# A seven-product matmul group: its running weight sum begun one group earlier, its third sum added on VectorE, and two blocks of small work given out in steps

## Chip, cores, metric

One core of a Trainium2 chip. The metric is the device time of one execution in microseconds (us). Before the change: 3050.57 us, the median of three runs (3047.31 to 3052.44).

## What is computed

Two consecutive layers of a decoder trunk on one sequence of 256 tokens, width 2048, in float32. What matters here, cut from the reference:

```python
h = x
for i in range(DEPTH):                       # 2 layers
    h = h + mixers[i](rmsnorm(h, attn_norms[i]))
    h = h + conv_ffn(rmsnorm(h, ffn_norm), w_up, conv_w, conv_b, w_down)
    h = h + ple_term(h, p[i], w_proj, gate_norm, w_gate)
return rmsnorm(h, final_norm)

def conv_ffn(hn, w_up, conv_w, conv_b, w_down):       # w_up (2048, 11264), w_down (5632, 2048)
    u = causal_dwconv(hn @ w_up, conv_w) + conv_b     # 3 taps over the tokens
    gate, up = jnp.split(u, 2, axis=-1)
    return (jax.nn.silu(gate) * up) @ w_down
```

Layer 0's mixer projects the normed input once and feeds two groups of heads: a gated delta rule, which needs per-head gates (`beta = sigmoid(b)`, `g = -exp(A_log) * softplus(a + dt_bias)` and its cumulative sums), and a latent attention, which needs a rotation table (`cos`, `sin` of positions times inverse frequencies). Layer 1's mixer is a retention. All weights are read once from HBM.

## The kernel before

**Matmuls.** A float32 product is made of float32r pieces: a 128x1024 piece of a weight is cast by ScalarE to `hi` (L186), VectorE makes `lo` = weight - `hi` (L187), and TensorE multiplies `hi` with both parts of the activation and `lo` with its high part. `load` (L162) brings 1 MB of weight with one or more DMAs on SP's queue into a tile of the pool `rawp`, which has four buffers (`RAWB`); `cut` (L174) makes `hi` and `lo` from it, in pools of four tiles each. A buffer comes free when both have been made. `gemm_b` (L250) makes a product with the weights stationary (L259, L264), `gemm_a` (L277) with the activations stationary (L288, L289, L294).

**Who orders the work.** The program is written as Python generators that yield after some matmuls each; `weave`, `turn` and the loops of the FFN interleave them. Small work is put in the queue `todo` with `later` (L207), and `turn` (L210), which each GEMM calls after every eight or sixteen matmuls, takes one entry from it; `behind` (L202) keeps the entry's TensorE instructions behind the last matmul issued. A planner then sets the order in which each engine's instructions stand, by this order as priority and by what is ready in its own simulation; it also gives out the buffers. On the chip each engine, SP's and GpSimd's DMA queues too, goes through its instructions in that fixed order and waits at each for its inputs and its buffer.

**The FFN** (`ffn`, L1021) cuts the 44 tiles of 128 hidden channels into six groups: 4, 8, 8, 8, 8, 8. For each group `up` makes the gate and the up-projection (`conv`: two `gemm_b` of 2 MB of `w_up` per pair of tiles) and writes their product into `xg` tiles, four for a group of eight (`xtile`, L120; the pool has 18). `down` then multiplies the group with its 1024 rows of `w_down` and adds into `h`. `down` of one group runs as filler inside `up` of the next: `up` gets a lead of `LAG` = 6 steps, and then `down` makes 0.85 steps for each of `up`. The last group's `down` runs alone.

For the four middle groups of each FFN, half of `down` (512 columns twice) is done by `seven` (L390): one level of Winograd's form of Strassen's algorithm. The 256 tokens, the group's 1024 hidden channels and the 1024 columns are each halved, and instead of eight products of halves there are seven, over sums of weight blocks and sums of activation blocks (`Forms`, L362). Call the weight blocks B11, B12 (upper half) and B21, B22 (lower half). Their sums are made by DMA: `put` (L394) copies a block, `plus` (L398) issues from GpSimd a DMA that adds a block to what is in the tile. Each is two DMAs of 512 KB.

- A *running sum* `run_t` lives in two `xg` tiles. `put` B11 and `plus` B12 come at the start of `seven` (L433, L434), which `down` reaches after the lead (`next(fast)`, L1071). Product one reads it; `plus` B22 (L440), product four reads it; `plus` B21 (L449), product seven reads it.
- The *third sum* `t3` takes a buffer of `rawp` (L450): `put` B12 and `plus` B22. Product six reads it.
- Products two, three and five read plain blocks (`fresh`, L406): B11, B21 and B22.

The other half of `down` (columns 1024 on) is the ordinary `gemm_a` (`slow`, L1072); one step of it alternates with two of `seven`.

**The start.** The last 1104 columns of layer 0's input projection are made in three GEMMs, `g3` = 0, 1, 2 (L619). At `g3` = 1 the positions, the gates' parameters and the constants are loaded. At `g3` = 2 the program issues, all at once and ahead of that GEMM: the gates (`gates`, L564), the norm of the compressed queries (`low_rank`, L609), and the rotation tables (`rope_tables`, L467). The transposes of the compressed queries (`gained`, L308) are queued as the third turn of that GEMM.

Of the kernel before, what the change touches and what calls it, by code (L numbers as in the profile page):

```python
# [21 lines left out]
P = 128  # L22
# [29 lines left out]
C_QN = 96  # L52
# [32 lines left out]
def trunk(ctx: ExitStack, tc: tile.TileContext, a: dict):  # L85
# [121 lines left out]
    def later(*steps):  # L207
        todo.extend(steps)

    def turn():  # L210
        if todo:
            behind(todo.popleft())
# [174 lines left out]
                return self.hi[q][n // 2][:, n % 2, k], self.lo[q][n // 2][:, n % 2, k]  # L387
            return at

    def seven(w, r0, c, tiles, forms):  # L390

        blocks = w[r0 : r0 + 8 * P, c * 512 : (c + 2) * 512].rearrange("(q h k p) (e n) -> q h e p k n", q=2, h=2, k=2, e=2)

        def put(dst, hh, e):  # L394
            for q in range(2):
                nc.sync.dma_start(dst[q], blocks[q, hh, e])

        def plus(dst, hh, e):  # L398
            for q in range(2):
                G.dma_start(dst[q], blocks[q, hh, e], accum_op=ALU.add)  # L400

        def slab():
            raw = rawp.tile([P, 4, 512], F32, tag="raw", name=nm("raw"))
            return [raw[:, 2 * q : 2 * q + 2] for q in range(2)]

        def fresh(hh, e):  # L406
            dst = slab()
            put(dst, hh, e)
            return dst

        def x(half, i):
            def at(q, k):
                return xl(tiles, 4 * q + 2 * half + k, i)
            return at

        def product(o, left, right, start):
            los = []
            for q in range(2):
                hi, lo = cut(right[q], 2, 512)
                los.append(lo)  # L420
                for k in range(2):
                    l = left(q, k)
                    T.matmul(o, l[0], hi[k], start=start and q + k == 0, stop=False, skip_group_check=True)  # L423
                    last_mm[0] = T.matmul(o, l[1], hi[k], start=False, stop=False, skip_group_check=True)  # L424
                yield
            for q in range(2):
                for k in range(2):
                    last_mm[0] = T.matmul(o, left(q, k)[0], los[q][k], start=False, stop=q + k == 2, skip_group_check=True)
            yield

        h11, h12, h21, h22 = h[0][c], h[0][c + 1], h[1][c], h[1][c + 1]
        run_t = [xtile().bitcast(F32).rearrange("p a b c -> p a (b c)") for _ in range(2)]
        put(run_t, 0, 0)  # L433
        plus(run_t, 0, 1)  # L434
        yield
        one = pb()
        yield from product(one, forms.left(0), run_t, True)
        V.tensor_sub(h22, h22, one)
        V.tensor_sub(h12, h12, one)
        plus(run_t, 1, 1)  # L440
# [12 lines left out]
        one = pb()  # L453
        yield from product(one, forms.left(3), fresh(1, 1), True)
        V.tensor_sub(h12, h12, one)
        yield from product(acc, forms.left(2), t3, False)
        V.tensor_sub(h22, h22, acc)
        V.tensor_add(h21, h21, acc)
        one = pb()
        yield from product(one, x(1, 1), run_t, True)  # L460
        V.tensor_add(h21, h21, one)

    def put_split(t, k, n, src):
# [1 line left out]
        V.tensor_sub(t[:, k : k + n, 1], src, t[:, k : k + n, 0].bitcast(F32))  # L465

    def rope_tables(inv, cos, sin, sign):  # L467
        big = 2.0 * math.pi * 4096.0
# [17 lines left out]
        turns_of(m, big)  # L486
        take(m, wide[:3])
        turns_of(n, 2.0 * math.pi)
        take(n, turn)
        take(m, wide[3:])  # L490
        turns_of(n, 2.0 * math.pi)
        take(n, turn)
        pi = 3.1415925
        V.tensor_scalar(ang, ang, pi, -pi, op0=ALU.min, op1=ALU.max)
        A.activation(sin, ang, AF.Sin)
        if sign is not None:
# [67 lines left out]
    def gates():  # L564
        def hh(t):
            return t.rearrange("p h i -> p i h")

        def sm():
            return small(16).rearrange("p (i h) -> p i h", i=NH)

        bl = ab[:, :, 8:16]
        e = sm()
        V.scalar_tensor_tensor(e, bl, -1.0, bl, op0=ALU.mult, op1=ALU.min)
        A.activation(e, e, AF.Exp)
        V.tensor_scalar(e, e, 1.0, None, op0=ALU.add)
# [4 lines left out]
        V.tensor_mul(hh(beta), num, e)  # L580
        x = sm()
# [4 lines left out]
        A.activation(e, na, AF.Exp)  # L586
        u = sm()
# [9 lines left out]
        V.scalar_tensor_tensor(lg, x, 0.0, lg, op0=ALU.max, op1=ALU.add)  # L597
        ea = small(8)
# [5 lines left out]
        T.matmul(ps[:, 16:32], M["sl"], gf, start=True, stop=True)  # L604
        A.activation(eg.rearrange("p h i -> p (h i)"), ps[:, 0:16], AF.Exp)
        A.activation(kdx.rearrange("p h i -> p (h i)"), ps[:, 16:32], AF.Exp)
        V.scalar_tensor_tensor(nbe, beta, -1.0, eg, op0=ALU.mult, op1=ALU.mult)
# [11 lines left out]
    for g3 in range(3):  # L619
        if g3 == 1:  # L620
# [5 lines left out]
            V.tensor_copy(posf, posi)  # L626
# [394 lines left out]
    def ffn(l, nf, nxt, aside=None):  # L1021
# [32 lines left out]
                        forms.add(*kept)  # L1054
                        kept = []

        def down(g0, g1, tiles, forms):
            r0, nk = g0 * P, g1 - g0

            def plain(cols):  # L1060
# [18 lines left out]

        groups = [(max(g - 4, 0), g + 4) for g in range(0, NFT, 8)]  # L1080
        prev = None
        for g0, g1 in groups:
# [362 lines left out]
```

## Time and profile before

| | |
|---|---|
| profiled execution: device time | 3052.88 us |
| its span (first to last instruction) | 3051.1 us |
| median of three runs | 3050.57 us |
| TensorE busy | 2925.1 us (96%) |
| VectorE / ScalarE / GpSimd busy | 2054.3 / 1540.0 / 141.3 us |
| mean granted TensorE clock | 0.976 |
| moved by DMA | 570.88 MB, mean 187 GB/s |
| the two FFNs' stretches with seven-product groups | about 667 to 1260 and 2313 to 2900 us |

In the profile PE is TensorE's matmuls, PEld its weight loads, DVE VectorE, ACT ScalarE, POOL GpSimd; SPq and POOLq are the DMA-issuing sequencers. An operand `hi<-xg` means that a tile of the pool `hi` was written from one of `xg`. In a timeline row the numbers are start and length in us; in brackets stands how long the engine was idle before, and what ended that. The granted clock is 1 or one half; a mean between them is a mixture.

### The profile page before, as it was taken

The numbers are of one execution on the slowest core, as the hardware profiler recorded it, in microseconds if no ns is written. First come the engines' busy times: TensorE is split into PE (matmuls) and PEld (weight loads), VectorE is DVE, ScalarE is ACT, GpSimd is POOL, SyncE is SP. The second block draws the span as 40 slices with busy tenths as digits, with TensorE's granted clock in tenths as the row PEclk, the third lists the DMA queues.
The fourth block names the chain that finished last, engine by engine and source line by source line (L and its number), as shares of the span: only waits on it lengthen the run. The fifth ranks groups of instructions, "written<-read, shape, count | busy, mean of one in ns | idle before, by whom it ended". The sixth has DMA issues, their size and how long they took to land.

```text
span 3051.1 us, 38714 instructions
## 1 busy us (share of the span) xinstructions
PE 2925.1 (96%) x15076; PEld 2489.3 (82%) x15076; DVE 2054.3 (67%) x2882; ACT 1540.0 (50%) x2185; POOL 141.3 (5%) x132
## 2 busy tenths in 40 slices
PE   8999999999998999999999999999999999999998
PEld 8899988877777777888888888888887777777787
DVE  6888858767676766756655555666676767676664
ACT  6666645544454544554444444444555545445454
POOL 0111100000000000000000000000000000001000
PEclk9999999999999999999999999999999999999999
DMA  6444355567676767655555555555567677777654
GB/s 207 144 126 135 121 194 193 189 177 207 196 219 192 214 195 212 199 180 188 182 182 183 195 182 187 180 183 187 180 194 206 192 209 204 204 210 204 203 180 152
DMA packets 414392, 570.88 MB, mean 187 GB/s; under 512 B 11008, under 2 KB 267136, under 8 KB 414208
## 3 DMA queue, kind: packets, MB, share of 16 engines
q1 hardware_dynamic: 393376, 530.05, 53.7%
q0 software_dynamic: 17408, 33.56, 6.5%
q10 hardware_dynamic: 3424, 4.79, 0.5%
q8 instruction: 118, 1.93, 0.3%
q14 instruction: 66, 0.54, 0.0%
HBM read 566.26 MB, written 2.10 MB: 186 GB/s over the span
## 4 chain that ended last, share of the span: by engine, by line
PE 86%; DMA 7%; DVE 4%; ACT 2%; issue 1%; POOL 0%; ACTq 0%; POOLq 0%; SPq 0%; DVEq 0%
PE pa L259 26%; PE pa L264 13%; PE pa L288 10%; PE pa L294 10%; PE pa L289 10%; DMA xg<-in_l_ffn_w_down_dram 3%; DMA raw<-in_l_ffn_w_up_dram 3%; DVE lo L187 2%; PE pb L289 2%; PE pb L288 2%; PE pb L294 2%; PE pb L423 2%; PE pb L704 2%; PE pb L424 1%; ACT hi L186 1%
## 5 line engine op out<-in xcount | busy, mean ns | idle before, releaser
L187 DVE TENSOR_TENSOR lo<-raw,hi 128x1024 fp32r<-128x1024 f32 (+3 forms) x1140 | 1194.4, 1075 | 668.3 <-ACT hi L186 420.6
L186 ACT CAST hi<-raw 128x1024 fp32r<-128x1024 f32 (+3 forms) x1140 | 1014.6, 930 | 1010.3 <-PE pa L289 326.6
L259 PE MATMUL pa<-xg,hi 128*128 128x512 f32 x3840 | 975.4, 400 | 45.6 <-ACT hi L186 45.6
L259 PEld LDWEIGHTS pa<-xg,hi 128*128 128x128 f32 x3840 | 724.5, 193 | 200.2 <-ACT hi L186 54.4
L288 PE MATMUL pa<-hi,xg 128*128 128x512 f32 (+1 forms) x1348 | 524.2, 389 | 5.1 <-ACT hi L186 5.0
L264 PEld LDWEIGHTS pa<-xg,lo 128*128 128x128 f32 x3840 | 495.0, 191 | 33.0 <-DVE lo L187 13.0
L289 PE MATMUL pa<-hi,xg 128*128 128x512 f32 (+1 forms) x1348 | 521.6, 387 | 0.3 <-DVE xg L313 0.2
L264 PE MATMUL pa<-xg,lo 128*128 128x256 f32 x3840 | 514.6, 284 | 0.2
L294 PE MATMUL pa<-lo,xg 128*128 128x512 f32 (+1 forms) x1348 | 332.7, 387 | 0.0
L288 PEld LDWEIGHTS pa<-hi,xg 128*128 128x128 f32 x1348 | 254.4, 189 | 55.0 <-ACT hi L186 5.9
L289 PEld LDWEIGHTS pa<-hi,xg 128*128 128x128 f32 x1348 | 254.4, 189 | 48.9 <-DVE xg L313 0.8
L294 PEld LDWEIGHTS pa<-lo,xg 128*128 128x128 f32 x1348 | 249.8, 188 | 47.6
L1039 DVE SCALAR_TENSOR_TENSOR t<-t,fp,t 128x255 f32<-128x255 f32 (+1 forms) x352 | 159.5, 480 | 61.5 <-ACT t L1037 57.7
L288 PE MATMUL pb<-hi,xg 128*128 128x512 f32 x348 | 139.8, 402 | 0.0
L289 PE MATMUL pb<-hi,xg 128*128 128x512 f32 x348 | 139.6, 401 | 0.0
L1037 ACT ACTIVATE t<-t,fp 128x256 f32<-128x256 f32 x176 | 96.0, 593 | 74.6 <-DVE t L274 74.6
L271 ACT COPY t<-pa 128x512 f32<-128x512 f32 x128 | 74.9, 585 | 94.9 <-PE pa L264 85.6
L400 POOL DMA_DIRECT2D xg<-in_l_ffn_w_down_dram x48 | 57.9, 1207 | 1284.5 <-DMA xg<-in_l_ffn_w_down_dram 559.7
L187 DVE TENSOR_TENSOR lo<-xg,hi 128x1024 fp32r<-128x1024 f32 x48 | 58.0, 1223 | 84.9 <-ACT hi L186 61.9
L423 PE MATMUL pb<-hi,t 128*128 128x512 f32 x128 | 57.1, 446 | 55.0 <-ACT hi L186 55.0
L156 POOL TENSOR_TENSOR small<-small,mhalf 128x1 f32<-128x1 f32 (+2 forms) x38 | 28.7, 754 | 1440.4 <-DVE small L1214 622.5
L186 ACT CAST hi<-xg 128x1024 fp32r<-128x1024 f32 x48 | 49.5, 1047 | 88.4 <-DMA xg<-in_l_ffn_w_down_dram 58.5
(281 smaller groups left out, 2335.3 us busy)
## 6 DMA issues: line engine op xcount, KB each, us to landing
raw<-in_l_ffn_w_up_dram SPq DMA_DIRECT2D x176, 1024.0 KB, 5.6
raw<-in_l_w_in_dram SPq DMA_DIRECT2D x128, 1024.0 KB, 5.2
raw<-in_l_ffn_w_down_dram SPq DMA_DIRECT2D x56, 1024.0 KB, 5.2
raw<-in_l_w_out_dram SPq DMA_DIRECT2D x44, 1024.0 KB, 5.2
raw<-in_l_ffn_w_down_dram SPq DMA_DIRECT2D x64, 512.0 KB, 5.6
raw<-in_l_ple_gate_dram SPq DMA_DIRECT2D x32, 1024.0 KB, 5.1
xg<-in_l_ffn_w_down_dram POOLq DMA_DIRECT2D x48, 512.0 KB, 7.3
xg<-in_l_ffn_w_down_dram SPq DMA_DIRECT2D x16, 512.0 KB, 6.1
```

The costliest lines, as they stand in the source:

```text
L186: last_cast[0] = A.copy(vo(hi)[:, c], vi(rk)[:, c])
L187: V.tensor_sub(vo(lo)[:, c], vi(rk)[:, c], vo(hi)[:, c].bitcast(F32))
L259: last_mm[0] = T.matmul(ps[:, j], wh, x2, start=first, stop=False)
L264: last_mm[0] = T.matmul(ps[:, j, :S], lo[k][:, j * P : (j + 1) * P], xr(tiles, c * 8 + k)[1], start=False, stop=c == 1 and k == 7)
L271: A.copy(u, ps[:, :, S:])
L288: T.matmul(o[i], xh, hi[k], start=begin and k0 + k == 0, stop=False)
L289: last_mm[0] = T.matmul(o[i], xw, hi[k], start=False, stop=False)
L294: last_mm[0] = T.matmul(o[i], xl(tiles, k0 + k, i)[0], lo[k], start=False, stop=end and k0 + k == nkb - 1)
L423: T.matmul(o, l[0], hi[k], start=start and q + k == 0, stop=False, skip_group_check=True)
L704: T.matmul(ps[:, u * P : (u + 1) * P], l[:, u], r[:, u], start=True, stop=True)
L1037: A.activation(y[:, j], u[:, j], AF.Identity, scale=fc(ct + 176), bias=fc(ct + 264))
L1039: V.scalar_tensor_tensor(y[:, j, lag:], u[:, j, : S - lag], fc(ct + (2 - lag) * 88), y[:, j, lag:], op0=ALU.mult, op1=ALU.add)
```

## The change

Four edits:

1. `run_t` becomes `total`, two `xg` tiles taken once per FFN and kept. Its `put` B11 and `plus` B12 for the next group are issued by a callback, `then`, at the end of `seven` for the present group, when product seven has been issued; in the plain first group, at its start. For the last group there is none.
2. `t3` is no longer made by an accumulating DMA. B12 is brought by a plain `fresh` after product five, and VectorE adds B22 to it, from the buffer that product five read.
3. `gates` and the rotation tables become generators with `yield`s; at `g3` = 1 they are put in `todo` in 5 and 9 steps (`stepwise`), with the copy of the positions between.
4. At `g3` = 2 the norm of the compressed queries becomes the first turn, and their transposes the sixth.

```diff
+    def stepwise(gen, n):
+        later(*[partial(next, gen, None)] * n)
...
+    class Quads:
+        def __init__(self, w, r0, c, total):
+            self.blocks = w[r0 : r0 + 8 * P, c * 512 : (c + 2) * 512].rearrange("(q h k p) (e n) -> q h e p k n", q=2, h=2, k=2, e=2)
+            self.c = c
+            self.total = total
+        def put(self, dst, hh, e):
+            for q in range(2):
+                nc.sync.dma_start(dst[q], self.blocks[q, hh, e])
+        def plus(self, hh, e):
+            for q in range(2):
+                G.dma_start(self.total[q], self.blocks[q, hh, e], accum_op=ALU.add)
+        def begin(self):
+            self.put(self.total, 0, 0)
+            self.plus(0, 1)
...
+    def running():
+        return [xtile().bitcast(F32).rearrange("p a b c -> p a (b c)") for _ in range(2)]
+
+    def seven(quads, tiles, forms, then):
...
-        run_t = [xtile().bitcast(F32).rearrange("p a b c -> p a (b c)") for _ in range(2)]
-        put(run_t, 0, 0)
-        plus(run_t, 0, 1)
-        yield
         one = pb()
         yield from product(one, forms.left(0), run_t, True)
...
-        plus(run_t, 1, 0)
-        t3 = slab()
-        put(t3, 0, 1)
-        plus(t3, 1, 1)
+        plus(1, 0)
         one = pb()
-        yield from product(one, forms.left(3), fresh(1, 1), True)
+        b22 = fresh(1, 1)
+        yield from product(one, forms.left(3), b22, True)
         V.tensor_sub(h12, h12, one)
+        t3 = fresh(0, 1)
+        for q in range(2):
+            V.tensor_add(t3[q], t3[q], b22[q])
         yield from product(acc, forms.left(2), t3, False)
...
         yield from product(one, x(1, 1), run_t, True)
+        then()
         V.tensor_add(h21, h21, one)
...
+            later(lambda: None, lambda: None)
+            stepwise(gates(), 5)
+            later(lambda: V.tensor_copy(posf, posi))
+            stepwise(rope_steps(cst[:, C_IMLA : C_IMLA + 1], cos_t, sin_t, cst[:, C_SIGN : C_SIGN + 1]), 9)
         if g3 == 2:
-            with tc.issue_after(last_cast[0].ins):
-                gates()
-                low_rank(cq)
             cqT = []
-            later(lambda: None, lambda: None, lambda: cqT.extend(gained(cq, C_QN)))
-            rope_tables(cst[:, C_IMLA : C_IMLA + 1], cos_t, sin_t, cst[:, C_SIGN : C_SIGN + 1])
+            todo.appendleft(partial(low_rank, cq))
+            todo.insert(5, lambda: cqT.extend(gained(cq, C_QN)))
...
             if forms is None:
+                then()
                 yield from plain(range(CG))
                 return
-            fast = seven(w_dn, r0, 0, tiles, forms)
-            next(fast)
+            fast = seven(quads, tiles, forms, then)
...
+        def following(g0):
+            if g0 + 8 < NFT:
+                if not total:
+                    total.extend(running())
+                quads.append(Quads(w_dn, g0 * P, 0, total))
+                quads[-1].begin()
...
-                behind_it = down(*prev)
+                behind_it = down(*prev, quads[-1] if quads else None, partial(following, g0))
```

More of the change, by code (lines that the diff above doesn't have):

```diff
@@ L388, in left, with fresh @@
             return at
-    def seven(w, r0, c, tiles, forms):
-        blocks = w[r0 : r0 + 8 * P, c * 512 : (c + 2) * 512].rearrange("(q h k p) (e n) -> q h e p k n", q=2, h=2, k=2, e=2)
-        def put(dst, hh, e):
+    class Quads:
[4 more added lines that the diff above has]
+        def put(self, dst, hh, e):
             for q in range(2):
-                nc.sync.dma_start(dst[q], blocks[q, hh, e])
-        def plus(dst, hh, e):
+                nc.sync.dma_start(dst[q], self.blocks[q, hh, e])
+        def plus(self, hh, e):
             for q in range(2):
-                G.dma_start(dst[q], blocks[q, hh, e], accum_op=ALU.add)
-        def slab():
+                G.dma_start(self.total[q], self.blocks[q, hh, e], accum_op=ALU.add)
+        def begin(self):
+            self.put(self.total, 0, 0)
+            self.plus(0, 1)
+        def fresh(self, hh, e):
             raw = rawp.tile([P, 4, 512], F32, tag="raw", name=nm("raw"))
[L404 to L408, printed above, removed]
-            return dst
+            dst = [raw[:, 2 * q : 2 * q + 2] for q in range(2)]
+            self.put(dst, hh, e)
+            return dst
+    def running():
+        return [xtile().bitcast(F32).rearrange("p a b c -> p a (b c)") for _ in range(2)]
+    def seven(quads, tiles, forms, then):
+        c, run_t, fresh, plus = quads.c, quads.total, quads.fresh, quads.plus
         def x(half, i):
@@ L439, in seven @@
         V.tensor_sub(h12, h12, one)
-        plus(run_t, 1, 1)
+        plus(1, 1)
         acc = pb()
@@ L467, in rope_tables, with rope_steps @@
     def rope_tables(inv, cos, sin, sign):
+        return run(rope_steps(inv, cos, sin, sign))
+    def rope_steps(inv, cos, sin, sign):
         big = 2.0 * math.pi * 4096.0
@@ L486, in rope_tables @@
         turns_of(m, big)
+        yield
         take(m, wide[:3])
+        yield
         turns_of(n, 2.0 * math.pi)
+        yield
         take(n, turn)
+        yield
         take(m, wide[3:])
+        yield
         turns_of(n, 2.0 * math.pi)
+        yield
         take(n, turn)
+        yield
         pi = 3.1415925
@@ L495, in rope_tables @@
         A.activation(sin, ang, AF.Sin)
+        yield
         if sign is not None:
@@ L580, in gates @@
         V.tensor_mul(hh(beta), num, e)
+        yield
         x = sm()
@@ L586, in gates @@
         A.activation(e, na, AF.Exp)
+        yield
         u = sm()
@@ L597, in gates @@
         V.scalar_tensor_tensor(lg, x, 0.0, lg, op0=ALU.max, op1=ALU.add)
+        yield
         ea = small(8)
@@ L604, in gates @@
         T.matmul(ps[:, 16:32], M["sl"], gf, start=True, stop=True)
+        yield
         A.activation(eg.rearrange("p h i -> p (h i)"), ps[:, 0:16], AF.Exp)
@@ L1055, in up, with down @@
                         kept = []
-        def down(g0, g1, tiles, forms):
+        def down(g0, g1, tiles, forms, quads, then):
             r0, nk = g0 * P, g1 - g0
@@ L1081, in ffn @@
         prev = None
+        total = []
+        def following(g0):
[4 more added lines that the diff above has]
+                quads[-1].begin()
+        quads = []
         for g0, g1 in groups:
```

1 line of the change is left out of this document (removed).

## The prediction

> **What bounds the kernel now.** I read the page first, then TensorE's waits, then the timeline around one wait of each kind. The page's first part says TensorE is the bound:
>
> ```profile
> PE 2925.1 (96%) x15076; PEld 2489.3 (82%) x15076; DVE 2054.3 (67%) x2882; ACT 1540.0 (50%) x2185; POOL 141.3 (5%) x132
> ...
> L187 DVE TENSOR_TENSOR lo<-xg,hi 128x1024 fp32r<-128x1024 f32 x48 | 58.0, 1223 | 84.9 <-ACT hi L186 61.9
> ```
>
> So a change that leaves TensorE's matmuls alone, as this one does, can win only the 4% in which TensorE stands still, and what a standstill costs afterwards. The waits of TensorE (total us, times, longest):
>
> ```profile
> PE pb L423 <- ACT hi L186: 55.0, 8, 7.6
> PE pa L259 <- ACT hi L186: 45.6, 8, 7.6
> PE pa L288 <- ACT hi L186: 5.0, 3, 2.0
> PE pb L308 <- DVE t L617: 2.8, 1, 2.8
> ```
>
> Two waits come eight times each, once per seven-product group (four groups in each of two FFNs), 100.6 us together. Each is followed by slow matmuls. I asked for the 8 us after each of the sixteen restarts (columns: length, busy time and count of PE, PEld, DVE, ACT, POOL, granted clock, DMA share, GB/s); first two and last two of 16 rows:
>
> ```profile
> 673.61:681.61 8.00, 8.00 (x23) 6.32 (x24) 2.34 (x2) 3.23 (x4) 1.20 (x1) 0.62 0.49 75
> 746.09:754.09 8.00, 8.00 (x24) 6.38 (x25) 3.65 (x6) 3.97 (x5) 0.00 (x0) 0.67 0.02 6
> ...
> 2769.15:2777.15 8.00, 8.00 (x29) 6.38 (x30) 2.34 (x2) 4.33 (x5) 1.20 (x1) 0.82 0.45 74
> 2841.14:2849.14 8.00, 8.00 (x23) 6.21 (x24) 4.34 (x7) 3.86 (x6) 0.00 (x0) 0.62 0.01 3
> ```
>
> The sixteen clocks sum to 10.70, so (16 - 10.70) x 8 us = 42.4 us of matmul time is lost: 20.7 after the first kind (eight clocks sum to 5.41), 21.7 after the second (5.29). Both waits with their slow clock cost 143.0 us, 17.9 per group.
>
> **The first wait: the running sum.** The timeline shows it (start, length, engine, line, idle time before):
>
> ```profile
> 781.13 2.36 DVE L187 TENSOR_TENSOR lo<-xg,hi 128x1024 fp32r<-128x1024 f32 x2 [1.65 <-issue]
> ...
> 791.03 0.37 SPq L167 DMA_DIRECT2D raw<-in_l_ffn_w_up_dram  x1
> ...
> 797.34 4.23 SPq L167 DMA_DIRECT2D raw<-in_l_ffn_w_up_dram  x2
> ...
> 807.44 0.97 SPq L396 DMA_DIRECT2D xg<-in_l_ffn_w_down_dram  x2
> ...
> 813.09 1.19 POOL L400 DMA_DIRECT2D xg<-in_l_ffn_w_down_dram  x1 [81.68 <-DMA xg<-in_l_ffn_w_down_dram]
> ...
> 823.14 1.04 ACT L186 CAST hi<-xg 128x1024 fp32r<-128x1024 f32 x1 [7.54 <-DMA xg<-in_l_ffn_w_down_dram]
> ...
> 824.23 0.80 PE L423 MATMUL pb<-hi,t 128*128 128x512 f32 x1 [7.16 <-ACT hi L186]
> ```
>
> The old group's last reader of the sum ends at 781.13 + 2.36 = 783.49. The new sum is put by SP only at 807.44. It needs 5.65 us until POOL may add (813.09), then 10.05 until ScalarE casts (823.14). TensorE had run dry at 824.23 - 7.16 = 817.07. ScalarE waits in order, so the casts behind it stand too.
>
> The change issues both put and add when the old group's last product is through. If SP takes the put behind its next load (791.03 + 0.37), the cast can begin at 791.4 + 5.65 + 10.05 = 807.1, 8.9 us before it must (817.07 - 1.04 = 816.03). Even behind the two loads that end at 801.57 it begins at 817.3, 1.2 us late. So the wait goes: 55.0 + 20.7 us. The number of transfers of this sum is unchanged; they move some 16 us forward, into a stretch whose loads are issued at a pace of 3 to 7 us. For the first group of each FFN the sum is begun under the plain four-tile group, a whole group early. The two xg tiles stay taken between groups: 8 norm tiles, 4 and 4 product tiles and these 2 make 18, the pool's size, as now while a group runs; I price that at nothing, covered by the old product tiles coming free at the same end of group. Without that cover the next group's first pair would wait for the last low matmuls, at most one step.
>
> **The second wait: the third sum's slab.**
>
> ```profile
> 720.91 7.09 SPq L396 DMA_DIRECT2D raw<-in_l_ffn_w_down_dram  x4
> ...
> 725.50 2.44 POOL L400 DMA_DIRECT2D raw<-in_l_ffn_w_down_dram  x2 [0.50 <-DMA raw<-in_l_ffn_w_down_dram]
> ...
> 734.29 22.63 SPq L167 DMA_DIRECT2D raw<-in_l_ffn_w_up_dram  x3
> ...
> 735.54 1.05 ACT L186 CAST hi<-raw 128x1024 fp32r<-128x1024 f32 x1 [1.80 <-DMA raw<-in_l_ffn_w_down_dram]
> ...
> 744.99 2.94 ACT L186 CAST hi<-raw 128x1024 fp32r<-128x1024 f32 x3 [5.81 <-DMA raw<-in_l_ffn_w_up_dram]
> ...
> 746.09 2.08 PE L259 MATMUL pa<-xg,hi 128*128 128x512 f32 x4 [5.69 <-ACT hi L186]
> ...
> 760.57 0.69 DVE L455 TENSOR_TENSOR t<-t,pb 128x512 f32<-128x512 f32 x1 [0.35 <-PE pb L428]
> ...
> 762.18 0.39 PE L423 MATMUL pb<-hi,t 128*128 128x512 f32 x1
> ```
>
> SP issues four halves from 720.91: the third sum's first block, then the block of product four. The third sum takes one of four raw buffers at 720.91 though its product starts at 762.18. So the next w_up load gets a buffer only at 734.29 and, among POOL's accumulating transfers, lands after 10.7 us (744.99). TensorE had run dry at 740.40.
>
> After the change the block of product four takes 720.91. That w_up load then takes the turn that the second pair of the four has now (they end at 720.91 + 7.09 = 728.00), about 727, and the accumulating transfer of 1 MB is gone. Even with 10.7 us it lands at 738, and with the 5.65 of above at 733: in time for 740.40 less a cast. The third sum's plain load comes two loads later, about 741, and lands by 752, before VectorE gets to it; the stretch before is shorter by the first wait, so by this measure VectorE gets there about 751. It is tight, and I take the wait as gone: 45.6 + 21.7 us.
>
> What comes in its place are sixteen adds of 128x1024. The subtraction of the page's second row is the same shape: 1.22 us each, 2.4 per group. They lie on VectorE:
>
> ```profile
> 673.61:824.23 150.62, 137.73 (x692) 115.56 (x692) 104.49 (x136) 73.95 (x91) 9.57 (x8) 0.94 0.71 203
> 2400.00:2450.00 50.00, 50.00 (x270) 42.63 (x270) 38.94 (x47) 27.38 (x33) 0.00 (x0) 1.00 0.68 222
> 500.00:550.00 50.00, 50.00 (x288) 44.21 (x289) 44.49 (x76) 28.40 (x38) 0.00 (x0) 1.00 0.57 188
> ```
>
> A group of 150.6 us becomes 150.6 - 17.9 = 132.7, and VectorE 106.9 of it, 81%; it has been 89% busy with TensorE full (third row). The DMA moves 150.62 us x 203 GB/s = 30.6 MB less 1.05, or 222 GB/s, what the second row carries without a gap. Neither becomes the bound on average.
>
> The adds can still stand in a chain. If VectorE takes them behind the subtraction at 760.57, ScalarE's cast can start at 760.57 + 0.69 + 1.22 (2.44 if the first cast waits for both adds), and TensorE's product at 763.5 (764.7) instead of 762.18: 1.4 (2.6) us idle. Behind the adds on VectorE wait the low parts of the w_up tiles, needed some microseconds later. If the adds slip ahead of the subtraction, it is zero. A short gap may or may not slow the clock:
>
> ```profile
> 62.47 0.69 PE L308 MATMUL pb<-ident,t 128*128 128x128 f32 x2 [2.83 <-DVE t L617]
> ...
> 62.47:70.47 8.00, 8.00 (x43) 7.94 (x44) 5.88 (x13) 3.88 (x10) 0.00 (x0) 0.82 0.38 121
> 93.00:101.00 8.00, 8.00 (x48) 7.16 (x48) 5.61 (x14) 6.22 (x12) 0.00 (x0) 1.00 0.44 134
> ```
>
> After 2.83 us the clock was 0.82 for 8 us (1.4 us lost), after the gap before 93.00 (VectorE's, 2.0 us) it was whole. So the bounds are 0 and 2.6 + 1.4 = 4.0 us per group; I take 0.7 (half of the shorter chain, as the order is open), 5.6 us in all. The Trainium skill ("TensorE: Matmul & The Clock Gate", HAM oscillation) counts only gaps above about 3.4 us as harmful to the clock. The 2.83 us row disagrees; by the rule the upper bound would be 2.6 and the sum's upper end 11 us lower.
>
> **Gates and tables in steps.** Today the chain into the wait at 62.47 is this:
>
> ```profile
> 58.13 1.28 ACT L605 ACT_TABLE_LOAD   x1
> ...
> 61.92 0.88 DVE L617 TENSOR_SCALAR t<-t,small 128x512 f32<-128x512 f32 x2 [0.82 <-POOL small L156]
> ...
> 66.39 1.52 PE L294 MATMUL pa<-lo,xg 128*128 128x368 f32 x8
> ...
> 70.42 1.51 PE L294 MATMUL pa<-lo,xg 128*128 128x368 f32 x8
> ```
>
> The gates come wholly before the tables, so this table load leaves the chain (1.28 us), and the transposes come three turns later, a step of 70.42 - 66.39 = 4.0 us. Together they cover 2.83 us: with the clock 4.3 us are won. No instruction is added. The gates' own matmuls move up about 6 us; if TensorE meets them before VectorE's result, up to that is lost (with the clock 7). Bounds: a gain of 9 (the 5.0 us of L288 partly too) and a loss of 3 net. I take 4.3, because the wait of 2.83 is the row that the moved steps touch.
>
> **Sum.** The profiled execution took 3052.9 us (span 3051.1), 2.3 above the median of 3050.6. 3052.9 - 143.0 - 4.3 + 5.6 = 2911.2, or 2909 as a median.
>
> **Rivals.**
> 1. *The second wait stays* at its size, because product four's block is now held until the adds and the buffers are as scarce. For it: three buffers are left for everything else in that stretch, and the load of the third sum lands close to need. Against: the starved w_up load moves ahead by a turn. 3052.9 - 55.0 - 20.7 - 4.3 = 2973, median 2971.
> 2. *The first wait stays*: SP takes the put as late as now, behind loads that wait for buffers (the row at 807.44 speaks for it); against, that the put can be issued four SP loads earlier. 3052.9 - 45.6 - 21.7 - 4.3 + 5.6 = 2987, median 2985.
> 3. *Slower*: the adds stop VectorE. If the third sum's put gets a buffer only when VectorE has reached the adds, VectorE waits for it to land (the row of four issues ends at 728.00, the cast of the last pair's first half starts at 735.54: 7.5 us), adds and casts 2.3, less 1.6 that TensorE has left: 8.2. Meanwhile no low part is made and no buffer freed, so the next w_up load comes late like today's, 10.7. With two slow restarts of 2.65: 24.2 us per group, 3052.9 - 143.0 - 4.3 + 194 = 3099, median 3097. It decides for slower from (143.0 + 4.3) / 8 = 18.4 us per group. Against: four buffers let SP run about two loads ahead.
> 4. *Nothing*: both transfers stay where they are in their queues and the waits keep their size: about 3050.
>
> **Chances.** Forecast 0.72. Its own range ends above at 2909 + 32 - 5.6 (the add chains) + 4.3 + 2.7 (the start's loss) = 2942. Below, the start gives 4.7 more, the adds 5.6, and the gaps between matmuls may close a little; their pitch is in these rows:
>
> ```profile
> 657.82 2.08 PE L264 MATMUL pa<-xg,lo 128*128 128x256 f32 x16
> ...
> 659.74 3.82 PE L259 MATMUL pa<-xg,hi 128*128 128x512 f32 x16
> ...
> 663.39 0.39 PE L288 MATMUL pb<-hi,xg 128*128 128x512 f32 x1
> ```
>
> (659.74 - 657.82) / 16 = 0.120 us for 256 columns, 3.65 / 16 = 0.228 for 512. A group's 692 matmuls (256 of the first kind in eight up-projections) take 256 x 0.120 + 436 x 0.228 = 130.1, 2.6 less than 132.7. Half of that in eight groups is 10 us: 2889. Rival 1 0.12, rival 2 0.07, rival 3 0.04, rival 4 0.05. For 8 in 10 the range reaches over the own range and rival 1: 2888 to 2975. This kernel's runs agree within 5 us, so 0.2% (6 us) is about what can be told: faster 0.72 + 0.12 + 0.07 = 0.91, same 0.05, slower 0.04.
>
> **What would show it.** Right: L423's wait in the list of TensorE's waits gone or near 0, and POOL's first add on the sum some 10 us or more before ScalarE's cast; L259's wait gone; a clock of 1.0 over both FFNs; groups of about 132 us; no accumulating transfer into raw; sixteen adds of 1.2 us. Wrong: a new wait of VectorE for the third sum's transfer, or a wait of L259 or L423 of over 3 us per group; L308 waiting for L617 still, or L603 waiting at all.

## The result, and the profile after

The changed kernel takes 2905.43 us (median of four runs, 2905.28 to 2905.79); the kernel before, on the same chip, 3051.51 (3047.31 to 3053.89). The ratio is 0.9523, interval 0.9506 to 0.9539: 146 us won. The forecast was 2909, range 2888 to 2975. The profiled execution of the changed kernel took 2905.5 us, span 2903.7. The edits shift the line numbers; of the names in the prediction, L259 is now L262, L264 is L267, L288 is L291, L294 is L297, L308 is L311, L423 is L438, L396 is L403, L400 is L407, L455 is L464, L617 is L645.

The first line of the page after:

```profile
PE 2879.7 (99%) x15076; PEld 2457.5 (85%) x15076; DVE 2067.7 (71%) x2898; ACT 1539.3 (53%) x2185; POOL 121.6 (4%) x116
```

TensorE does the same 15076 matmuls in 2879.7 us instead of 2925.1, and of the span 2903.7 - 2879.7 = 24.0 us are left over instead of 3051.1 - 2925.1 = 126.0. So of the 147.4 us between the two profiled executions 102.0 are standstill and 45.4 are matmuls that no longer run at the half clock. VectorE has sixteen instructions more, GpSimd sixteen fewer.

TensorE's waits after (total us, times, longest):

```profile
PE pa L291 <- ACT hi L186: 7.1, 2, 5.4
PE pb L726 <- DVE t L845: 1.6, 1, 1.6
PE pa L267 <- DVE lo L187: 1.2, 4, 0.4
```

Neither of the two waits that came eight times each (L423 and L259 before) is in the list. The only large one left, 5.4 us, is at the start of the program, and it is longer than what stood there before. The first FFN's stretch, after (columns: stretch, length, busy time and count of PE, PEld, DVE, ACT, POOL, granted clock, DMA share, GB/s), with one group's period in the first row:

```profile
759.95:892.11 132.16, 132.07 (x694) 111.53 (x693) 106.28 (x138) 73.84 (x90) 7.19 (x6) 1.00 0.75 223
667.00:1260.00 593.00, 592.19 (x3048) 497.85 (x3047) 460.23 (x588) 329.63 (x418) 25.93 (x22) 1.00 0.72 215
```

and the same stretch before:

```profile
667.00:1260.00 593.00, 543.48 (x2714) 454.62 (x2713) 408.13 (x522) 290.64 (x352) 36.12 (x30) 0.94 0.71 203
```

TensorE stands still 0.8 us of 593, where it stood 49.5, and its clock is whole. A group has gone from 150.6 to 132.2 us; VectorE is busy 106.3 of them (80%), and the DMA moves 223 GB/s. The second FFN, which now starts earlier, looks the same (after):

```profile
2253.00:2766.00 513.00, 512.17 (x2674) 431.92 (x2674) 411.27 (x528) 285.00 (x351) 24.07 (x20) 1.00 0.75 221
```

The timeline of the changed kernel shows how both sums arrive (start, length, engine, line, idle time before):

```profile
706.57 0.89 SPq L403 DMA_DIRECT2D raw<-in_l_ffn_w_down_dram  x2
712.70 7.63 SPq L167 DMA_DIRECT2D raw<-in_l_ffn_w_up_dram  x2
724.96 0.88 SPq L403 DMA_DIRECT2D raw<-in_l_ffn_w_down_dram  x2
...
729.27 1.22 DVE L467 TENSOR_TENSOR raw<-raw,raw 128x1024 f32<-128x1024 f32 x1 [0.30 <-DMA raw<-in_l_ffn_w_down_dram]
730.65 1.22 DVE L467 TENSOR_TENSOR raw<-raw,raw 128x1024 f32<-128x1024 f32 x1 [0.16 <-DMA raw<-in_l_ffn_w_down_dram]
...
739.05 0.68 DVE L464 TENSOR_TENSOR t<-t,pb 128x512 f32<-128x512 f32 x1
...
740.28 0.39 PE L438 MATMUL pb<-hi,t 128*128 128x512 f32 x1
...
758.70 2.36 DVE L187 TENSOR_TENSOR lo<-xg,hi 128x1024 fp32r<-128x1024 f32 x2 [1.97 <-issue]
...
759.95 1.50 SPq L403 DMA_DIRECT2D xg<-in_l_ffn_w_down_dram  x2
...
764.09 1.20 POOL L407 DMA_DIRECT2D xg<-in_l_ffn_w_down_dram  x1 [47.01 <-DMA xg<-in_l_ffn_w_down_dram]
...
790.06 1.05 ACT L186 CAST hi<-xg 128x1024 fp32r<-128x1024 f32 x1 [1.53 <-issue]
...
794.45 0.40 PE L438 MATMUL pb<-hi,t 128*128 128x512 f32 x1
```

From the top: product four's block is put at 706.57, and the next w_up load follows after 6.1 us. The third sum's plain load is issued at 724.96; VectorE adds to each half as it lands (729.27, 730.65), and TensorE begins product six only at 740.28, 8.4 us after the second add ends. The running sum: its last readers are the two subtractions from 758.70, and SP puts the first half of the next group's block at 759.95, when the first of the two has ended; GpSimd adds at 764.09, 26.0 us ahead of ScalarE's cast at 790.06.

### The profile page after: what moved, and what is told of

Read it like the earlier page. It is cut to its first block, busy times and chain, and to the rows that moved or that the text cites. A ratio compares the mean times of both kernels' runs of the same rounds, so it can differ in the third digit from the quotient of the medians.

```text
span 2903.7 us, 38666 instructions
## 1 busy us (share of the span) xinstructions
PE 2879.7 (99%) x15076; PEld 2457.5 (85%) x15076; DVE 2067.7 (71%) x2898; ACT 1539.3 (53%) x2185; POOL 121.6 (4%) x116
## 4 chain that ended last, share of the span: by engine, by line
PE 92%; DVE 4%; DMA 1%; issue 1%; ACT 1%; POOL 0%; SPq 0%; ACTq 0%; POOLq 0%; DVEq 0%
PE pa L262 28%; PE pa L267 15%; PE pa L291 10%; PE pa L292 10%; PE pa L297 10%; PE pb L292 2%; PE pb L291 2%; PE pb L297 2%; DVE lo L187 2%; PE pb L732 2%; PE pb L438 2%; PE pb L439 1%; PE pb L443 1%; PE pb L311 1%; DMA raw<-in_l_ffn_w_down_dram 1%
## 5 line engine op out<-in xcount | busy, mean ns | idle before, releaser
L262 PE MATMUL pa<-xg,hi 128*128 128x512 f32 x3840 | 950.8, 393 | 0.0
L262 PEld LDWEIGHTS pa<-xg,hi 128*128 128x128 f32 x3840 | 705.8, 188 | 146.5 <-ACT hi L186 8.3
L291 PE MATMUL pa<-hi,xg 128*128 128x512 f32 (+1 forms) x1348 | 523.5, 389 | 7.2 <-ACT hi L186 7.1
L267 PEld LDWEIGHTS pa<-xg,lo 128*128 128x128 f32 x3840 | 495.0, 191 | 34.6 <-DVE lo L187 14.6
L267 PE MATMUL pa<-xg,lo 128*128 128x256 f32 x3840 | 514.7, 284 | 1.5 <-DVE lo L187 1.2
L297 PE MATMUL pa<-lo,xg 128*128 128x512 f32 (+1 forms) x1348 | 332.6, 387 | 0.0
L291 PEld LDWEIGHTS pa<-hi,xg 128*128 128x128 f32 x1348 | 253.9, 188 | 56.9 <-ACT hi L186 7.7
L297 PEld LDWEIGHTS pa<-lo,xg 128*128 128x128 f32 x1348 | 249.8, 188 | 47.5
L292 PE MATMUL pb<-hi,xg 128*128 128x512 f32 x348 | 135.9, 390 | 0.0
L291 PE MATMUL pb<-hi,xg 128*128 128x512 f32 x348 | 135.7, 390 | 0.0
L407 POOL DMA_DIRECT2D xg<-in_l_ffn_w_down_dram x48 | 57.9, 1206 | 1185.4 <-DVE t L1067 395.5
L297 PE MATMUL pb<-lo,xg 128*128 128x512 f32 x348 | 92.4, 391 | 0.0
L275 DVE TENSOR_TENSOR t<-t,pa 128x512 f32<-128x512 f32 x128 | 87.1, 680 | 3.8 <-ACT t L274 3.8
L316 DVE SCALAR_TENSOR_TENSOR xg<-pb,par,xg 128x256 fp32r<-128x256 f32 x136 | 59.7, 479 | 35.9 <-ACT xg L315 35.5
```

Source lines behind the costliest of these rows:

```text
L262: last_mm[0] = T.matmul(ps[:, j], wh, x2, start=first, stop=False)
L267: last_mm[0] = T.matmul(ps[:, j, :S], lo[k][:, j * P : (j + 1) * P], xr(tiles, c * 8 + k)[1], start=False, stop=c == 1 and k == 7)
L275: V.tensor_add(u, u, ps[:, :, :S])
L291: T.matmul(o[i], xh, hi[k], start=begin and k0 + k == 0, stop=False)
L292: last_mm[0] = T.matmul(o[i], xw, hi[k], start=False, stop=False)
L297: last_mm[0] = T.matmul(o[i], xl(tiles, k0 + k, i)[0], lo[k], start=False, stop=end and k0 + k == nkb - 1)
```

## The experiments

Each kernel has its own runs of the kernel before beside it (medians 3049.8, 3049.5 and 3049.8 us on the three chips).

### The parts one by one

First the changed kernel again, and beside it, on one chip, one kernel with edit 1 alone (the sum a group ahead), one with edit 2 alone (the third sum on VectorE), one with edits 3 and 4 alone (steps). With edit 1 alone, the third sum is made as before:

```diff
+        t3 = fresh(0, 1)
+        for q in range(2):
+            G.dma_start(t3[q], quads.blocks[q, 1, 1], accum_op=ALU.add)
         one = pb()
-        b22 = fresh(1, 1)
-        yield from product(one, forms.left(3), b22, True)
+        yield from product(one, forms.left(3), fresh(1, 1), True)
         V.tensor_sub(h12, h12, one)
-        t3 = fresh(0, 1)
-        for q in range(2):
-            V.tensor_add(t3[q], t3[q], b22[q])
```

Edit 2 alone is the same exchange the other way round, made in the kernel before.

> The changed kernel itself, on the chip of the next three. 2905 us, both kinds of FFN wait at zero.

> The kernel before with the running sum begun a group ahead and nothing else changed (the third sum by accumulating DMA, gates and tables all at once). Theory, two waits with causes of their own: the first product's wait on the sum (55.0 us of idle time, 20.7 of slow clock) goes, the second (45.6 + 21.7) stays: 3051 - 76 = 2975 us. Rival, the first wait is also a rest in which the loads catch up, so the second grows by as much as the first was: over 3020 us. Rival, the DMA is simply full and both waits shrink in part: L423's wait still some 20 us.

> The kernel before with only the third sum changed: plain load after product five, two VectorE adds. Theory: the second wait goes (45.6 + 21.7 us) and the first stays: 3051 - 67 = 2984 us. Rival, the second wait is an echo of the first (buffers run down while the sum's transfers go first): L259 still waits 20 us or more, time over 3010.

> The kernel before with only the gates and rotation tables in steps. The prediction said 4.3 us of gain. Having seen the changed kernel's trace, theory now: the 2.8 us wait at 62 us goes with its slow clock, but the gates' two ScalarE table loads come ahead of the first casts of the second GEMM and a wait of about 5.4 us stands at 36 us instead of 1.9: a gain of 0 to 4 us, 3047 to 3051 us. Rival, the new wait at 36 us has to do with something else: it is absent here and the gain is 4 to 6 us.

Measured: the changed kernel 2905.96 us (ratio 0.9529, interval 0.9515 to 0.9544), edit 1 alone 2977.23 (0.9764, 0.9749 to 0.9778), edit 2 alone 2982.91 (0.9782, 0.9768 to 0.9797), the steps alone 3047.19 (ten runs; 0.9992, 0.9982 to 1.0001). Against 3049.83 before, they win 72.6, 66.9 and 2.6 us: 142.1 together, and the whole change wins 143.9. So the parts add up, and neither wait was hiding behind the other. The waits say the same. Edit 1 alone:

```profile
PE pa L262 <- ACT hi L186: 47.6, 9, 7.6
PE pa L291 <- ACT hi L186: 4.9, 3, 1.9
PE pb L311 <- DVE t L644: 2.8, 1, 2.8
```

Edit 2 alone:

```profile
PE pb L423 <- ACT hi L186: 52.9, 8, 7.8
PE pa L288 <- ACT hi L186: 4.0, 3, 1.9
PE pb L308 <- DVE t L618: 2.8, 1, 2.8
```

Each leaves the other's wait at its old size. The interval of the steps alone reaches to 1.0001: their 2.6 us can't be told from nothing by these runs.

### What made the third sum's slab cost 67 us

The old way did two things at once: it held a raw buffer from early on, and it sent accumulating transfers through the stretch in which TensorE waits for a w_up load. Two kernels take them apart. One is the changed kernel with its plain load issued early (buffer held, no accumulating transfer):

```diff
+        t3 = fresh(0, 1)
         b22 = fresh(1, 1)
         yield from product(one, forms.left(3), b22, True)
         V.tensor_sub(h12, h12, one)
-        t3 = fresh(0, 1)
         for q in range(2):
             V.tensor_add(t3[q], t3[q], b22[q])
```

The other is the changed kernel with accumulating transfers at the late place (no buffer held):

```diff
-        b22 = fresh(1, 1)
-        yield from product(one, forms.left(3), b22, True)
+        yield from product(one, forms.left(3), fresh(1, 1), True)
         V.tensor_sub(h12, h12, one)
         t3 = fresh(0, 1)
         for q in range(2):
-            V.tensor_add(t3[q], t3[q], b22[q])
+            G.dma_start(t3[q], quads.blocks[q, 1, 1], accum_op=ALU.add)
```

> The changed kernel, but the plain load of the third sum's first block is issued ahead of product five's block, where the third sum's slab was taken before; VectorE adds as changed, no accumulating DMA into it. Theory, the second wait came from a raw buffer taken long before its use: the wait of L259 is back with 4 to 7 us per group, 2905 + 45 to 67 = 2950 to 2972 us. Rival, it came from the accumulating DMA (1 MB more, and its place among the transfers): no wait, 2905 to 2910 us.

> The changed kernel, but the third sum is made by an accumulating DMA again, at its new late place. Theory (buffer taken long): no wait of L259 for a w_up load as before; the sum is complete about 11 to 13 us after its load is issued at 725 us, about 738, a cast before its use at 740.3, so 0 to 3 us per group, 2905 to 2940 us, and any wait is L423's, for the sum. Rival (accumulating DMA): the wait of L259 is back, 2950 us or more.

Measured: 2913.11 us for the early load (0.9551, 0.9537 to 0.9566) and 2908.85 for the late accumulating transfers (0.954, 0.9526 to 0.9554). Neither alone brings the 67 us back. The early load should have cost 44 to 66 us by the theory that the buffer decides, and costs some 7 (2913.11 - 2905.96, medians of two chips); that theory falls. Its rival, 2905 to 2910 us, is missed too, by 3 us. The accumulating transfers alone, at their new place, cost no more than some 3 us. That kernel changes two things at once, since the late place also frees the buffer early; none here sends them at the old place without holding a buffer.

The stretch with edit 1 alone, which has both (timeline; the first row is the third sum's put together with product four's):

```profile
711.85 7.08 SPq L403 DMA_DIRECT2D raw<-in_l_ffn_w_down_dram  x4
725.23 7.18 SPq L167 DMA_DIRECT2D raw<-in_l_ffn_w_up_dram  x2
...
735.83 2.94 ACT L186 CAST hi<-raw 128x1024 fp32r<-128x1024 f32 x3 [5.72 <-DMA raw<-in_l_ffn_w_up_dram]
...
736.93 2.07 PE L262 MATMUL pa<-xg,hi 128*128 128x512 f32 x4 [5.60 <-ACT hi L186]
```

and with the early plain load:

```profile
707.06 7.12 SPq L403 DMA_DIRECT2D raw<-in_l_ffn_w_down_dram  x4
720.44 16.68 SPq L167 DMA_DIRECT2D raw<-in_l_ffn_w_up_dram  x3
...
727.64 2.95 ACT L186 CAST hi<-raw 128x1024 fp32r<-128x1024 f32 x3 [2.32 <-DMA raw<-in_l_ffn_w_up_dram]
...
728.74 1.20 PE L262 MATMUL pa<-xg,hi 128*128 128x512 f32 x4 [2.20 <-ACT hi L186]
```

In both the w_up load is issued 13.4 us after the put (in the changed kernel 6.1), so the buffer is as late in the one as in the other. TensorE is dry at the same place, 736.93 - 5.60 - 711.85 = 19.5 us after the put, and 728.74 - 2.20 - 707.06 = 19.5. What differs is how long the load takes until ScalarE may cast: 10.6 us with accumulating transfers in its way, 7.2 without. 13.4 + 7.2 is 1.1 us past that point, 13.4 + 10.6 is 4.5, and the first cast's 1.1 us comes on top of both: 2.2 and 5.6, the waits in the rows.

Is it that they add, or that their bytes are in the way? A third kernel takes edit 1 alone and has GpSimd's transfers copy B22 into the tile, with the same bytes at the same place; its third sum is B22 alone instead of B12 + B22:

```diff
-            G.dma_start(t3[q], quads.blocks[q, 1, 1], accum_op=ALU.add)
+            G.dma_start(t3[q], quads.blocks[q, 1, 1])
```

> The kernel with only the running sum begun a group ahead (2977 us, second wait 47 us), but the two GpSimd DMAs into the third sum's slab copy B22 instead of adding it, so the third sum is B22 alone and the output is not the reference's: the same bytes at the same place, without the add. Theory, the late w_up load in that place took 10.5 us instead of 7.1 because accumulating transfers are in its way: the second wait falls to 0 to 2 us per group as with VectorE's adds, 2911 to 2930 us. Rival, the extra 1 MB at that moment is what delays it: wait of L259 unchanged, about 6 us per group, 2970 to 2980 us.

Measured: 2953.05 us (0.9687, 0.9671 to 0.9704), between the two expectations. Its stretch:

```profile
709.64 7.09 SPq L403 DMA_DIRECT2D raw<-in_l_ffn_w_down_dram  x4
723.03 19.20 SPq L167 DMA_DIRECT2D raw<-in_l_ffn_w_up_dram  x3
...
731.18 2.94 ACT L186 CAST hi<-raw 128x1024 fp32r<-128x1024 f32 x3 [3.26 <-DMA raw<-in_l_ffn_w_up_dram]
...
732.27 2.06 PE L262 MATMUL pa<-xg,hi 128*128 128x512 f32 x4 [3.14 <-ACT hi L186]
```

Again 13.4 us from put to load, and now 8.2 us to the cast. TensorE's waits at this line come to 28.1 us, against 47.6 with adding and 7.0 with the early plain load. So of the time that TensorE stands still here, about half is due to the second megabyte and half to its being added. In device time the second megabyte weighs more: copying in place of adding saves 24.2 us (2977.23 to 2953.05), and going on to the early load 39.9 (to 2913.11, some 2.6 of it from the steps, which only that kernel has; the three ran on three chips). The slow matmuls make the difference: TensorE is busy 2902.1 us with adding, still 2897.9 with copying, and 2881.9 with the early load. The transfers themselves differ likewise (DMA issues: how many, KB each, median us from issue to landing). Adding, in the kernel with edit 1 alone:

```profile
raw<-in_l_ffn_w_down_dram POOLq DMA_DIRECT2D x16, 512.0 KB, 10.6
```

Copying, the same bytes at the same place:

```profile
raw<-in_l_ffn_w_down_dram POOLq DMA_DIRECT2D x16, 512.0 KB, 7.5
```

Adding at the late place of the changed kernel:

```profile
raw<-in_l_ffn_w_down_dram POOLq DMA_DIRECT2D x16, 512.0 KB, 6.7
```

At the crowded place adding takes 3.1 us longer than copying; at the late place even adding takes only 6.7. The price is that of the place as much as of the kind.

### How much room the adds have

The adds were priced at 0.7 us per group. Two kernels give VectorE more of them: each add is followed, once or twice, by a subtraction and an add of the same block: three or five passes over the tile in place of one. With five:

```diff
         for q in range(2):
             V.tensor_add(t3[q], t3[q], b22[q])
+            for _ in range(2):
+                V.tensor_sub(t3[q], t3[q], b22[q])
+                V.tensor_add(t3[q], t3[q], b22[q])
```

> The changed kernel with three VectorE passes per half of the third sum instead of one (add, subtract, add): 4.9 us more of VectorE per group, in the chain of the third sum. Theory: the adds run as soon as the load lands, 729.3 to 731.8 us in the first group, 8 us ahead of the subtraction at 739.05 and the cast after it; 4.9 us more fits: 2905 to 2908 us. Rival, the adds lie on the path: 8 x 4.9 = 39 us more, 2944 us.

> As the run before with five passes: 9.8 us more of VectorE per group. Theory: the sum is done at about 741.6 us, 2.4 us after the cast should start, and the low parts behind it are late too: 1 to 5 us per group with the clock, 2913 to 2945 us. Rival, VectorE has room anyway: 2905 us. Rival, on the path from the first pass: 8 x 9.8 = 78 us more, 2983 us.

Measured: 2911.24 us with three (0.9549, 0.9533 to 0.9565), 2952.71 with five (0.9684, 0.967 to 0.9699). With three, 4.9 us of extra VectorE work in each of eight groups (39 us) cost about 5 in all (against 2905.96, on another chip), a little more than the 0 to 3 expected. With five the time lies above the expected range (2913 to 2945): 9.8 us per group bring the wait of product six:

```profile
PE pb L438 <- ACT hi L186: 28.2, 8, 4.2
```

One group of the kernel with five (timeline):

```profile
730.87 1.23 DVE L467 TENSOR_TENSOR raw<-raw,raw 128x1024 f32<-128x1024 f32 x1 [0.16 <-DMA raw<-in_l_ffn_w_down_dram]
...
738.12 1.23 DVE L469 TENSOR_TENSOR raw<-raw,raw 128x1024 f32<-128x1024 f32 x1
739.26 0.69 DVE L464 TENSOR_TENSOR t<-t,pb 128x512 f32<-128x512 f32 x1
739.86 1.23 DVE L470 TENSOR_TENSOR raw<-raw,raw 128x1024 f32<-128x1024 f32 x1
740.99 2.36 DVE L469 TENSOR_TENSOR raw<-raw,raw 128x1024 f32<-128x1024 f32 x2
743.26 2.36 DVE L470 TENSOR_TENSOR raw<-raw,raw 128x1024 f32<-128x1024 f32 x2
...
745.66 2.94 ACT L186 CAST hi<-raw 128x1024 fp32r<-128x1024 f32 x3 [2.47 <-DVE raw L470]
...
746.75 0.50 PE L438 MATMUL pb<-hi,t 128*128 128x512 f32 x1 [4.18 <-ACT hi L186]
```

The extra passes were put behind other work of VectorE, from 738.12 on, and the cast waits for the two adds that end at 745.62. Of the 46.8 us that five passes cost, 28.2 are this wait and 18.2 slower matmuls (TensorE busy 2897.9 us in place of 2879.7). The single adds of the changed kernel end at 731.87, and the cast for product six need begin only about one us before 740.28, so they have some 7 us to spare per group. The three passes do not simply fill this spare time: there too the extra ones begin only at 737.71, the first half is ready at 740.68, and its cast begins at 740.76. They cost little because sixteen matmuls of the up-projection (L267, from 740.09) stand ahead of product six in that kernel, which starts at 742.00.

### The start

In the changed kernel TensorE waits 5.44 us where it waited 1.86 before. The timeline there:

```profile
31.33 0.56 ACT L576 ACTIVATE t<-pa,small 128x352 f32<-128x352 f32 x1
...
32.44 1.28 ACT L621 ACT_TABLE_LOAD   x1
...
33.97 1.28 ACT L626 ACT_TABLE_LOAD   x1
...
35.37 3.28 ACT L186 CAST hi<-raw 128x368 fp32r<-128x368 f32 x8
...
35.91 0.67 PE L291 MATMUL pa<-hi,xg 128*128 128x368 f32 x1 [5.44 <-ACT hi L186]
```

The gates, though queued in five turns from the second GEMM's third on, run on ScalarE ahead of that GEMM's first cast, with two table loads: as soon as the first GEMM's columns are copied out (L576), everything the gates need is there, and the planner places by readiness. The turns bind only TensorE's instructions. Before, the gates stood one GEMM later and were bound behind the last cast issued. So one kernel binds the steps likewise:

```diff
-            stepwise(gates(), 5)
+            gate = gates()
+            def held():
+                with tc.issue_after(last_cast[0].ins):
+                    next(gate, None)
+            later(*[held] * 5)
```

and another, on top, issues the second GEMM's first casts ahead of the copies out of the first:

```diff
+        if g3 == 0:
+            second = gemm_a(w_in, 0, KB, 4096 + 368, 368, X)
+            next(second)
         for i in range(NH):
             if g3 == 0:
```

> The changed kernel, but each of the five steps of the gates also stands behind the last ScalarE cast issued so far. Theory: the 5.4 us wait at 36 us is the two table loads of the gates ahead of the second GEMM's first casts; held back, the wait falls to about 1.9 us as before the change and the slow clock after it (2.1 us) may go: 2900 to 2904 us. Rival, the casts are late for another reason (the copies out of the first GEMM, the loads): wait unchanged, 2905 us.

> The run before, and the second GEMM's first four casts issued ahead of the copies out of the first GEMM. Theory: the 1.9 us that is left at 34 to 36 us is these copies (four on ScalarE, about 1.4 us); it goes to under 0.5 us: 1 to 4 us below the run before. Rival, the weight of the second GEMM is not there yet: no gain.

Measured: 2903.23 us (2902.14 to 2905.53; ratio 0.9522, 0.9508 to 0.9536) and 2898.60 (2897.69 to 2901.17; 0.9507, 0.9493 to 0.9521). The waits at L291 with the gates held:

```profile
PE pa L291 <- ACT hi L186: 4.1, 2, 2.2
```

and with the casts first as well:

```profile
PE pa L291 <- ACT hi L186: 1.9, 1, 1.9
```

Both lists hold another wait at the same line, in the first GEMM at about 17 us: 2.20 us with the gates held, 1.87 with the casts first. Held gates bring the 5.44 back to 1.86 us, and the clock over the 8 us after it is 1.00 where it was 0.73 in the changed kernel; the casts take the 1.86 too. The last is some 7 us below the changed kernel, the fastest version here, and 4.6 below the held gates, where 1 to 4 were expected; the wait that went is 1.86 of it. The intervals of the ratios overlap (0.9507 against 0.9529 and 0.9523), since the runs of the kernel before vary by more than this; the times do not: 2897.69 to 2901.17 here, 2905.28 to 2906.53 in the changed kernel's eight runs, though on different chips. That the held gates alone gain (2.2 to 2.7 us) is less sure, as their slowest run, 2905.53, lies among those.

## Why the prediction was right, and where it was not

**The first wait.** Right in mechanism and size. Priced at 75.7 us (55.0 standing, 20.7 slow), measured alone 72.6. The step said that SP would take the put behind its next load, 7.9 us after the last reader's end; it took it as soon as the half in question had been read. GpSimd adds 4.1 us later (5.65 was used), and from there 26.0 us pass until the cast, where the sum was said to need 10.05: some 16 us to spare, where 8.9 were worked out. The new place was never tight.

**The second wait.** Right in size: 67.3 us priced, 66.9 measured alone, and this with the adds in it, for which 5.6 us were to be taken off. In its mechanism the prediction named two causes, the buffer and the accumulating transfers, but reasoned that the load's move ahead would do even if the load still took 10.7 us. The early plain load answers a different half: the buffer as late as ever, and the wait all but gone (7.0 us of 47.6), since the load then takes 7.2 us. With the buffer as late as that, it takes the slow load as well. The half that the prediction relied on, the move ahead alone, was not run by itself; by the numbers above it would do, since 6.1 + 10.6 us and a cast of 1.1 make 17.8, less than the 19.5 at which TensorE runs dry. The prediction's rival 1, the wait staying at its size because a buffer is held, is what that kernel tests hardest, and it falls there as well as in the changed kernel.

One size was off. The prediction counts on the clock of the kernel before, where product four's block is put at 720.91; in the changed kernel that is 706.57, so the steps have to be compared from there. The third sum's load was to be issued 20 us after that put ("about 741"), and is issued after 18.4. It was to land 11 us later ("by 752"), as slowly as the load among the accumulating transfers; the last half's add starts 5.7 us later. VectorE was to reach the subtraction after 30 us and reaches it after 32.5. So the sum is done 8.4 us ahead of product six, and is not "tight": the landing time was the number that was wrong.

**The adds.** This term was mis-sized: 5.6 us taken, bounds 0 to 4.0 per group, and the trace shows zero. The question left open, whether they fall behind or ahead of the subtraction, has its answer in the timeline: ahead, by some 7 us. Three passes still cost only about 0.7 us per group, though they reach past the subtraction; five cost (2952.71 - 2905.96) / 8 = 5.8. The chain that was feared exists, but single adds stay some 7 us clear of it. VectorE at 80% and the DMA at 223 GB/s came out as worked (81%, 222), and neither binds.

**Gates and tables.** The wait of 2.83 us went, with its slow clock (1.00 from 55 to 75 us after), as predicted. The step that failed is the loss side: it was looked for where TensorE would meet the gates' matmuls ahead of VectorE's result, and it came on ScalarE, ahead of the second GEMM's casts, where the wait grew from 1.86 to 5.44 us. The prediction's upper bound had that wait at L288 shrinking. Net, the steps alone give 2.6 us, with zero inside the interval, of the 4.3 taken.

**The sum.** 3052.9 - 143.0 - 4.3 + 5.6 = 2911.2 was the forecast for a profiled execution; it took 2905.5. The difference of 5.7 us is the size of the adds' term. The two ways of losing time came out as priced: 102.0 us of standstill went and 45.4 of slow matmuls, where 103.4 (100.6 and 2.8) and 43.8 (42.4 and 1.4) were counted. What the start fell short (some 1.7 us) and what other short waits changed is too small to be told apart by these runs. Of the signs named, all those for "right" are there: no L423 wait, no L259 wait, clock 1.00, groups of 132.2 us, no accumulating transfer into raw, sixteen adds of 1.2 us. Of those for "wrong", none is: VectorE waits 0.30 and 0.16 us for the third sum's transfer. The wait that grew at the start was not among the signs.

## What to carry to other kernels

A wait that returns in every group can cost twice, once standing and once in slow matmuls after, as all sixteen did in the kernel before, and the trace gives both; for both sums edited here those two numbers together gave the gain within 4 us. When a load is late, ask of its two halves separately, when it got its buffer and how long it took from issue, and which other transfers run beside it: either half alone can be harmless. An order given as "turns" binds only the engine it is written for; for the others see what is ready early, and bind them too.

## What was not expected of the hardware

A transfer that adds into its tile landed 10.6 us after issue (median), and one that copied the same 512 KB at the same place 7.5. Beside it, the w_up load that TensorE needed took 10.6 us to its cast, 8.2 beside the copy, and 7.2 with neither. The Trainium skill ("DMA: Bandwidth & Descriptors", SDMA does more than copy) lists the elementwise add as a compute unit in line with the stream and gives no price for it; here it has one.

Gaps of the same length did not always slow the clock. The 8 us after a gap of 2.20 us, in the kernel with the gates held:

```profile
16.96:24.96 8.00, 8.00 (x52) 7.64 (x53) 6.21 (x14) 8.00 (x23) 0.00 (x0) 1.00 0.92 306
```

and after a gap of 1.87 us at the same matmul, in the kernel with the casts first:

```profile
16.48:24.48 8.00, 8.00 (x40) 7.71 (x41) 5.43 (x12) 6.69 (x19) 0.00 (x0) 0.79 0.86 293
```

The shorter gap lost (1 - 0.79) x 8 = 1.7 us, the longer none. Even the same gap of 1.86 us ahead of the second GEMM was followed by 0.79 in the kernel before (34.29 to 42.29) and by 1.00 with the gates held (33.12 to 41.12). The Trainium skill ("TensorE: Matmul & The Clock Gate", What's actually happening) says that the activity window runs freely, and that the moment at which the clock changes depends on where in the window the first matmul lands. That would fit these rows, but no run here varies the place alone. The figure of about 3.4 us that the Trainium skill ("TensorE: Matmul & The Clock Gate", HAM oscillation) gives for a harmful gap does not fit them as a limit: 1.87 and 2.83 us were harmful here, and the 2.20 beside them was not.
